# An FFN's output product two feature tiles behind its input product, in place of one

## The chip, the cores and the metric

The kernel runs on one core of a Trainium2 chip. TensorE (PE) multiplies, VectorE (DVE) and ScalarE (ACT) do the elementwise work, GpSimd (POOL) a few small things, and SyncE (SP) issues the loads. The metric is the device time of one execution in microseconds; lower is better.

## What is computed

Two layers of a decoder trunk over 256 tokens of width 1024, in float32. Each layer is an FFN, a mixer and a second FFN, each between two norms:

```
def swiglu(x, w_in, w_out):
    gate, up = jnp.split(x @ w_in, 2, axis=-1)      # w_in 1024 x 5632
    return (jax.nn.silu(gate) * up) @ w_out         # w_out 2816 x 1024
...
    h = swiglu(rms_norm(x, g[0]), ffn_w_in[layer, 0], ffn_w_out[layer, 0])
    x = x + 0.5 * rms_norm(h, g[1])
    ...                                             # mixer, then the second FFN in the same way
```

The first layer's mixer is a Mamba-2 scan beside forgetting attention, the second layer's a gated linear recurrence. So there are six phases: FFN, hybrid mixer, FFN, FFN, recurrent mixer, FFN (phases 0 to 5). The change touches the four FFNs only.

## The kernel before

The tokens are two tiles of 128. An FFN has 22 feature tiles of 128 (0 to 21). To keep float32's precision, every weight and activation is split into two parts that the fast matmul form takes exactly: a high part, made by ACT as a cast, and a low part, made by DVE as a difference. Every product is then made of three partial products.

Weights come in slabs of 512 KB: two per feature tile for the input product (below I17a, I17b and so on, from `in_ffn_in`), one for its output product (O17, from `in_ffn_out`). SP loads a slab into one of four `raw` buffers; ACT casts it into `w` (L252), DVE makes the low part (L253), and then the `raw` buffer is free for another load. Slabs are asked for in the order of first use, up to 7 slabs ahead.

The tensor engine takes its work in the order of a plan, `ffn_plan` (L42). After three tiles that are done token tile by token tile ("A"), the plan goes feature tile by feature tile. The input product of tile f, below B(f), is 32 matmuls plus their narrower companions into two PSUM buffers of the ring `rot`, which has four: the gate half first, then the up half. The output product O(f) adds tile f's part to the accumulators `side`: 12 matmuls for both token tiles, but only 6, for the first token tile, from tile 15 on, whose second token tile waits until the end (`DEFER`). Behind B(f), the chain of tile f (L530 to L541) runs on ACT and DVE: add the two parts of the gate half (`half` L267 on ACT, `sg` L268 on DVE), SiLU (`sg` L536, ACT), add the up half (`half`, `up`), multiply (`up` L538, DVE), and split the result into `hid` (L285, first ACT, then DVE). Only then can O(f) run.

In the plan, B(f) is followed by O(f-1). So the chain of f-1 has the time of one B to finish. The order on TensorE is that of the plan; on ACT and DVE a scheduler orders the casts of slabs among the chains' instructions, and each engine then works through its queue in that order, waiting at its head.

Of the kernel before, what the change touches and what calls it, by code (L numbers as in the profile page):

```python
# [8 lines left out]
F32 = mybir.dt.float32  # L9
# [7 lines left out]
P = 128          # partitions; also the rows of a token tile  # L17
NT = 2           # token tiles
DM = 1024
KT = DM // P     # contraction tiles of the model width  # L20
DFF = 2816
NF = DFF // P    # feature tiles of an FFN
HEADS = 16       # SSD heads of 64 channels
FOX = 8          # attention heads of 128 channels
EPS = 1e-6
NEG = -1e30
SLAB = 1024      # weight columns of one slab, per partition

NA = 3           # FFN feature tiles computed token tile by token tile at a phase's start
DEFER = 7        # last contraction tiles whose second token tile comes at a phase's end  # L30
LATE = {"hyb": 5, "rec": 6}  # last slabs of a mixer's output product that the phase's own pool holds
URGENT = 200     # priority of the first FFN tiles' vector work over the splits
WARM = 5         # products of ones before the first gain product: the tensor engine's clock comes up
LOOKAHEAD = {"ffn": 7, "hyb": 6, "rec": 6}     # slabs split ahead of their use

# lags in us of tensor-engine work before a product whose operand other engines still make
# [5 lines left out]
def ffn_plan(ph):  # L42
    if ph:
        plan = [("A", ph, f, t) for t in range(NT) for f in range(NA)]
    else:
        plan = [("A", ph, f, t) for f in range(NA) for t in range(NT)]
    pend, late = list(range(NA)), []

    def out(f):
        plan.append(("O", ph, f, 0))  # L50
        if f < NF - DEFER:
            plan.append(("O", ph, f, 1))
        else:
            late.append(f)

    for f in range(NA, NF):
        plan.append(("B", ph, f))
        for _ in range(2 if len(pend) > 1 else 1):
            out(pend.pop(0))
        pend.append(f)  # L60
    plan.append(("O", ph, late.pop(0), 1))
    plan += [("O", ph, NF - 1, 0), ("END", ph, 0)]
    late.append(NF - 1)
    if ph < len(PHASES) - 1:
        return plan + [("O", ph, f, 1) for f in late] + [("END", ph, 1)]
    return plan + [("O", ph, f, 1, h) for h in range(2) for f in late] + [("END", ph, 1)]
# [43 lines left out]
def hybrid_trunk(ctx: ExitStack, tc: tile.TileContext, x_in, norm_g, ffn_in, ffn_out,  # L110
# [59 lines left out]
    start_pool = tc.tile_pool(name="start", bufs=1)  # L170
    begin = start_pool.__enter__()
    g_row = begin.tile([P, DM], F32, name="g_row")   # rows that count: the first
# [47 lines left out]
    def is_late(key):  # L220
        """held until a phase's end: out of the phase's own pool"""
        what = PHASES[key[1]][0]
        return key[0] == "O" and (what == "ffn" or key[2] >= {"hyb": 16, "rec": 8}[what] - LATE[what])

# [5 lines left out]
    def behind(ins, firsts):  # L230
        """ins queues after the given instructions of its engine"""
        for h in firsts:
            if h.ins.engine == ins.ins.engine:
                tc.add_manual_dep(ins.ins, h.ins.name, mybir.DependencyInfo(
                    mybir.DependencyClass.NoSync, mybir.DependencyReason.DATA), reason="norms and splits in turn")
        return ins
# [27 lines left out]
    def halves(dst, ps):  # L264
        """dst = the two halves of ps together"""
# [4 lines left out]
    def mm_wide(ps, steps):  # L270
        """ps[:, 0:256] and ps[:, 256:512] add up to the sum of stationary^T moving, but for lo times lo;
        steps: (stationary hi, stationary lo, moving hi and lo, moving hi)"""
# [17 lines left out]
    def rstd_of(dst, ms, weight):  # L290
        """dst = weight * (mean square + EPS) ** -0.5, per token; ms holds halves of the mean square / weight ** 2"""
# [17 lines left out]
    def pre_norm(ph, t, xT, lag):  # L309
        """normalise token tile t of the residual, transpose it and split it: the input of phase ph"""  # L310
# [26 lines left out]
    def finish(ph, t, acc, weight):  # L337
        """residual update by token tile t of a phase's output, then the next phase's input"""
# [27 lines left out]
    def first_norms(xT):  # L366
        """pre_norm of the first phase: the gain is laid on all partitions by the tensor engine, and the transposes
        scale by the tokens' factors; every engine works in the order of emission"""
# [62 lines left out]
    def out_step(accs, k, t, n, act_hl, w, halves=(0, 1)):  # L431
        """accs[t][half] += act[k]^T w[k] for token tile t"""
# [10 lines left out]
    def b_one(xT, w, m=P):  # L443
        """[feature, token] of one column tile of m features"""
# [11 lines left out]
    def a_one(xT, t, s):  # L456
        """[token, column] of token tile t for 256 columns held in two slabs"""
# [12 lines left out]
    def b_tile(xT, s, off):  # L470
        """[feature, token] of the feature tile at column off of two slabs, in two halves"""
# [8 lines left out]
    def a_tile(xT, t, s):  # L480
        """[token, column] of token tile t for 256 columns held in two slabs, in two halves"""
# [11 lines left out]
    def run_ffn(ph, plan, xT, weight, hid):  # L493
        n_hid = DEFER + 2
# [55 lines left out]
    def softplus(dst, u, n, pool_):  # L550
        """dst = max(u, 0) + log(1 + exp(-|u|)), the log by its atanh series in z = e / (2 + e) <= 1/3"""
# [14 lines left out]
    def conv(src, wts, dst):  # L566
        """dst = causal convolution over the tokens of src[channel, token], taps wts[:, 0:4], bias wts[:, 4]"""
# [6 lines left out]
    def over(ap, n):  # L574
        """the same [partition, a] values for n positions of a new last axis"""
        return ap.unsqueeze(2).broadcast_to([P, ap.shape[1], n])

    def each(ap, n):
        """the same [partition, a] values for n positions of a new middle axis"""
        return ap.unsqueeze(1).broadcast_to([P, n, ap.shape[1]])  # L580

# [1 line left out]
    def run_hyb(ph, plan, xT, mp):  # L583
# [6 lines left out]
        cs = mp.tile([P, 64], F32, name="cs")               # running sums of the log decays  # L590
# [4 lines left out]
        at_pool = tc.tile_pool(name="at", bufs=1)           # until the last attention head  # L595
        at = at_pool.__enter__()
        upper = at.tile([P, P], F32, name="upper")          # 1 where partition <= column
        mask3 = at.tile([P, 3 * P], F32, name="mask3")      # causal | all | causal
# [7 lines left out]
        sd_pool = tc.tile_pool(name="sd", bufs=1)           # until the last SSD head  # L606
# [3 lines left out]
        # half the convolution, so that silu(y) = (1 + tanh(y / 2)) * (y / 2)  # L610
# [9 lines left out]
        d = sd.tile([P, NT, 24], F32, name="d")             # log decay per token: 16 SSD heads, 8 forget gates  # L620
# [9 lines left out]
        def gates(praw):  # L630
# [17 lines left out]
            # per token: columns 0:24 tile 0, 24:48 tile 1 (forget gates over both), 48:64 the SSD total of tile 0  # L648
# [8 lines left out]
            # the same with tokens along the free axis, to be laid on every partition by way of DRAM  # L657
# [8 lines left out]
        def weights_cb():  # L666
            """masked C B^T of each group and token tile, and B by token for tile 0"""
# [14 lines left out]
        def ssd(g):  # L682
            """the scan of the group's eight heads, the skip, the gate and the grouped norm"""
# [49 lines left out]
            # y holds twice the gated value, hence 4 EPS  # L733
# [71 lines left out]
        for op in plan:  # L805
# [21 lines left out]
            elif kind == "Z":  # L827
# [3 lines left out]
                # twice silu(z) = (1 + tanh(z / 2)) z  # L831
# [23 lines left out]
    def run_rec(ph, plan, xT, mp):  # L855
        gt = mp.tile([P, 8, 256], F32, name="gt")
        lr_pool = tc.tile_pool(name="lr", bufs=1)           # until the last block's gates are made
        lr = lr_pool.__enter__()
        rv = lr.tile([P, 8, 8], F32, name="rv")             # taps 0:4, conv bias, b_a, b_x, lambda
# [9 lines left out]
        dve.tensor_scalar(ls, ls, -4.0, None, op0=ALU.mult)  # half of 8 log sigmoid(lambda)  # L869
# [3 lines left out]
        def turn(c, t, ps):  # L873
            """two channel tiles of the recurrent branch from [token, channel]"""
# [12 lines left out]
        def lru(n0):  # L887
            """four blocks of channels"""
# [6 lines left out]
            for j in range(4):  # L895
# [5 lines left out]
                # sigmoid(s) = (1 + tanh(s / 2)) / 2  # L901
                act.activation(r[:, j, :], pr[:, 0:256], func=AF.Tanh, scale=0.5, bias=hb[:, n, 0:1])
                act.activation(i[:, j, :], pi[:, 0:256], func=AF.Tanh, scale=0.5, bias=hb[:, n, 1:2])
                dve.tensor_scalar(r[:, j, :], r[:, j, :], 1.0, ls[:, n:n + 1], op0=ALU.add, op1=ALU.mult)   # log a
                dve.scalar_tensor_tensor(i[:, j, :], i[:, j, :], 1.0, c[:, j, :], op0=ALU.add, op1=ALU.mult)
            act.activation(a, r, func=AF.Exp)
            # 1 - a^2 = (1 + a^2) tanh(-log a); half its root goes with 2 sigmoid
# [9 lines left out]
            # both groups' roots, then both groups' gates: a function table is loaded once for each  # L917
# [65 lines left out]
def _arrays(inp):  # L983
# [5 lines left out]
    w = a["ffn_w_in"].reshape(L, 2, 2, 4, P, 2, NF, P)          # l i kh k4 p gu f c  # L989
# [4 lines left out]
    def cols(m):                                                # column tiles, contraction split over partitions  # L994
# [3 lines left out]
    def wide(m):                                                # 256 columns in two halves of the contraction  # L998
# [6 lines left out]
    chan = lambda m, n: m.reshape(-1, n, P).transpose(2, 1, 0)  # channel tiles on partitions  # L1005
# [40 lines left out]
```

## Time and profile before

| | |
|---|---|
| time, median of 3 runs | 1071.39 us (1068.6 to 1071.75) |
| profiled execution, first to last instruction | 1069.3 us |
| its own time beside the span | not given apart; the median is 2.1 us above the span |
| TensorE busy | 1045.1 us (98%) |
| VectorE busy | 719.5 us (67%) |
| ScalarE busy | 602.9 us (56%) |
| DMA, mean over the span | 183 GB/s |

A busy TensorE is not TensorE at its peak: matmuls overlap, and a throttled clock makes them longer while the engine counts as busy. So the start times of successive products say more than the busy share.

### The profile page before, as it was taken

How to read it: one execution, taken by the hardware profiler on the slowest of the kernel's cores; microseconds unless marked ns; L12 is line 12 of the kernel's file. 1: busy time of each engine (PE TensorE's matmuls, PEld its weight loads, DVE VectorE, ACT ScalarE, POOL GpSimd, SP SyncE). 2: the span in 40 equal slices, each digit the busy share in tenths (PEclk: the TensorE clock that was granted, in tenths of full speed). 3: DMA queues.
4: the chain of work that ended last, by engine and by line, in shares of the span. 5: the costliest groups of instructions: out<-in, count | busy, mean ns of one | idle time of the engine just before them, and what ended most of it. 6: DMA issues, size and time to landing. Idle time of an engine off the chain costs nothing.

```text
span 1069.3 us, 16048 instructions
## 1 busy us (share of the span) xinstructions
PE 1045.1 (98%) x6084; PEld 912.1 (85%) x6084; DVE 719.5 (67%) x1156; ACT 602.9 (56%) x1060; POOL 24.6 (2%) x60
## 2 busy tenths in 40 slices
PE   8999999999999999999999999999999999999997
PEld 7788887999999988888887888888799878888876
DVE  7766556579888767855566675655669868655643
ACT  7655445465465556744555565445559857545531
POOL 1000000100000001000000100000010010000000
PEclk9999999999999999999999999999999999999999
DMA  7866565265645463866656285656535447665511
GB/s 269 298 227 196 188 195 171 82 219 186 202 149 168 134 226 104 289 198 197 192 181 197 83 291 185 195 193 194 185 116 178 142 154 244 232 196 193 180 59 39
DMA packets 55745, 195.90 MB, mean 183 GB/s; under 512 B 6972, under 2 KB 8148, under 8 KB 55668
## 3 DMA queue, kind: packets, MB, share of 16 engines
q1 hardware_dynamic: 52464, 190.04, 54.6%
q10 hardware_dynamic: 3204, 4.84, 1.4%
q8 instruction: 47, 0.77, 0.3%
q14 instruction: 30, 0.25, 0.1%
HBM read 193.78 MB, written 1.07 MB: 182 GB/s over the span
## 4 chain that ended last, share of the span: by engine, by line
PE 33%; DMA 30%; DVE 16%; ACT 10%; issue 8%; POOL 1%; POOLq 0%; DVEq 0%; ACTq 0%; SPq 0%
DMA raw<-in_ffn_out_dram 25%; PE rot L133 20%; PE side L133 12%; DVE w L253 10%; ACT w L252 7%; DMA raw<-in_ffn_in_dram 5%; DVE sg L268 2%; ACT junk L304 1%; DVE c L571 1%; PE rot L137 1%; DVE up L268 0%; POOL r L293 0%; DVE xn L320 0%; DMA raw<-in_rec_cols_dram 0%; DVE sc L921 0%
## 5 line engine op out<-in xcount | busy, mean ns | idle before, releaser
L253 DVE TENSOR_TENSOR w<-raw,w 128x1024 fp32r<-128x1024 f32 (+1 forms) x349 | 424.2, 1219 | 234.5 <-ACT w L252 232.7
L133 PE MATMUL rot<-xT,w 128*128 128x256 f32 (+1 forms) x3512 | 579.9, 324 | 1.3 <-DVE sg L268 1.3
L133 PEld LDWEIGHTS rot<-xT,w 128*128 128x128 f32 x3512 | 511.5, 190 | 62.0 <-DVE sg L268 1.7
L252 ACT CAST w<-raw 128x1024 fp32r<-128x1024 f32 (+1 forms) x349 | 364.8, 1049 | 220.7 <-DMA raw<-in_ffn_out_dram 177.2
L133 PE MATMUL side<-w,hid 128*128 128x512 f32 x1056 | 256.3, 393 | 8.5 <-ACT hid L285 8.4
L133 PEld LDWEIGHTS side<-w,hid 128*128 128x128 f32 x1056 | 197.3, 188 | 50.3 <-ACT hid L285 9.9
L133 PE MATMUL rot<-w,xT 128*128 128x256 f32 (+1 forms) x768 | 118.8, 313 | 0.0
L133 PEld LDWEIGHTS rot<-w,xT 128*128 128x128 f32 x768 | 105.6, 190 | 9.5 <-DVE w L253 0.3
L267 ACT COPY half<-rot 128x256 f32<-128x256 f32 x176 | 63.9, 363 | 31.8 <-PE rot L133 31.8
L285 ACT CAST hid<-up 128x256 fp32r<-128x256 f32 x76 | 30.9, 407 | 46.0 <-DVE up L538 46.0
L268 DVE TENSOR_TENSOR sg<-rot,half 128x256 f32<-128x256 f32 x100 | 41.9, 419 | 18.3 <-ACT half L267 18.2
L536 ACT ACTIVATE sg<-sg 128x256 f32<-128x256 f32 x76 | 31.8, 418 | 29.6 <-DVE sg L268 29.6
L133 PE MATMUL side<-w,os 128*128 128x512 f32 x192 | 46.2, 396 | 0.0
L133 PEld LDWEIGHTS side<-w,os 128*128 128x128 f32 x192 | 35.6, 188 | 7.9
L268 DVE TENSOR_TENSOR up<-rot,half 128x256 f32<-128x256 f32 x76 | 31.8, 418 | 9.0 <-ACT half L267 9.0
L285 DVE TENSOR_TENSOR hid<-up,hid 128x256 fp32r<-128x256 f32 x76 | 31.9, 420 | 8.5 <-ACT hid L285 8.5
L538 DVE TENSOR_TENSOR up<-sg,up 128x256 f32<-128x256 f32 x76 | 32.2, 424 | 2.0
L292 POOL TENSOR_SCALAR r<-ms 128x1 f32<-128x1 f32 x24 | 7.3, 302 | 886.6 <-ACT junk L304 881.8
L352 DVE TENSOR_TENSOR xn<-side,g_post 128x512 f32<-128x512 f32 x24 | 16.5, 691 | 15.3 <-ACT junk L304 14.9
L320 DVE SCALAR_TENSOR_TENSOR xn<-x,r,g_pre 128x512 f32<-128x512 f32 x20 | 14.1, 749 | 16.9 <-POOL r L293 16.9
L304 ACT ACTIVATE junk<-side 128x512 bf16<-128x512 f32 x24 | 14.3, 597 | 17.0 <-PE side L133 16.2
L304 ACT ACTIVATE junk<-x 128x512 bf16<-128x512 f32 x20 | 12.6, 632 | 19.5 <-DVE x L355 19.3
(195 smaller groups left out, 514.4 us busy)
## 6 DMA issues: line engine op xcount, KB each, us to landing
raw<-in_ffn_in_dram SPq DMA_DIRECT2D x176, 512.0 KB, 4.5
raw<-in_ffn_out_dram SPq DMA_DIRECT2D x88, 512.0 KB, 4.5
raw<-in_hyb_cols_dram SPq DMA_DIRECT2D x36, 512.0 KB, 4.0
raw<-in_hyb_out_dram SPq DMA_DIRECT2D x16, 512.0 KB, 3.5
raw<-in_hyb_v_dram SPq DMA_DIRECT2D x8, 512.0 KB, 3.6
raw<-in_rec_a_dram SPq DMA_DIRECT2D x8, 512.0 KB, 4.8
raw<-in_rec_cols_dram SPq DMA_DIRECT2D x8, 512.0 KB, 4.3
raw<-in_rec_out_dram SPq DMA_DIRECT2D x8, 512.0 KB, 3.6
```

Source lines behind the costliest of these rows:

```text
L133: pe.matmul(ps, lhsT=lhsT, rhs=rhs, start=start, stop=stop)
L137: pe.transpose(ps, src, ident)
L252: splits[:] = [behind(act.copy(w[:, 0, c], raw[:, c]), hold)]
L253: splits.append(behind(dve.tensor_tensor(w[:, 1, c], raw[:, c], w[:, 0, c].bitcast(F32), op=ALU.subtract), hold))
L267: act.copy(tmp, ps[:, 256:512])
L268: dve.tensor_tensor(dst, ps[:, 0:256], tmp, op=ALU.add)
L285: return act.copy(hi, src), dve.tensor_tensor(lo, src, hi.bitcast(F32), op=ALU.subtract)
L304: behind(act.activation(junk, src, func=AF.Square, scale=1.0 / (32.0 * weight), accum_out=ms[:, h:h + 1]), firsts)
L320: dve.scalar_tensor_tensor(xn[h], xt[:, cols], r, state["g_pre"][:, cols], op0=ALU.mult, op1=ALU.mult)
L352: behind(dve.tensor_tensor(hg[h], acc[h], state["g_post"][:, cols], op=ALU.mult), firsts)
L536: act.activation(sg, sg, func=AF.Silu)
L538: dve.tensor_tensor(up, sg, up, op=ALU.mult)
```

## The change

The plan lets `BEHIND` tiles, here 2, wait between input and output product: B(f) is followed by O(f-2). Ahead of the last steps, one more output product (that of tile 20) stands after the last input product. The ring of `hid` tiles grows by two buffers (9 pairs to 10). The rest of the diff only drops comments.

```
+BEHIND = 2
...
     for f in range(NA, NF):
         plan.append(("B", ph, f))
-        for _ in range(2 if len(pend) > 1 else 1):
+        for _ in range(2 if len(pend) > BEHIND else 1):
             out(pend.pop(0))
         pend.append(f)
+    while len(pend) > 1:
+        out(pend.pop(0))
     plan.append(("O", ph, late.pop(0), 1))
...
     def run_ffn(ph, plan, xT, weight, hid):
-        n_hid = DEFER + 2
+        n_hid = DEFER + BEHIND + 1
```

As slabs are asked for in the order of first use, each output slab also moves one tile back in the loads: the order after I18b is O16, I19a, I19b, O17, and at the end I21b, O19, O20, O21. Nothing moves outside the FFNs.

TensorE in phase 5, from the end of B(18) (`rot`) over the output product behind it (`side`) to the start of B(19). Before; hid_10337 and hid_10338 are the two parts of tile 17:

```order
L133 MATMUL rot_10379<-xT_8882,w_10216 128x512
L133 MATMUL side_9260<-w_10221,hid_10337 128x512 x2
L133 MATMUL side_9260<-w_10221,hid_10338 128x512
L133 MATMUL side_9261<-w_10221,hid_10337 128x512 x2
L133 MATMUL side_9261<-w_10221,hid_10338 128x512
L133 MATMUL rot_10431<-xT_8882,w_10274 128x512
```

And in the changed kernel, where hid_10251 and hid_10252 are tile 16:

```order
L136 MATMUL rot_10368<-xT_8882,w_10199 128x512
L136 MATMUL side_9260<-w_10204,hid_10251 128x512 x2
L136 MATMUL side_9260<-w_10204,hid_10252 128x512
L136 MATMUL side_9261<-w_10204,hid_10251 128x512 x2
L136 MATMUL side_9261<-w_10204,hid_10252 128x512
L136 MATMUL rot_10420<-xT_8882,w_10257 128x512
```

The product after B(18) now reads the tile whose chain began one B earlier; tile 17 (now hid_10326) is first read after B(19).

ACT in phase 5, from tile 16's last instruction to tile 17's. Before; raw_10426 is slab O20, raw_10410 I21a, raw_10479 O21, raw_10421 I21b; half_10329 and half_10333 are the gate and up half of tile 17:

```order
L285 CAST hid_10268<-up_10259 128x256
L267 COPY half_10329<-rot_10293 128x256
L252 CAST w_10428<-raw_10426 128x1024
L536 ACTIVATE sg_10327<-sg_10327 128x256
L252 CAST w_10412<-raw_10410 128x1024
L252 CAST w_10481<-raw_10479 128x1024
L267 COPY half_10333<-rot_10310 128x256
L252 CAST w_10423<-raw_10421 128x1024
L285 CAST hid_10337<-up_10328 128x256
```

In the changed kernel, with raw_10415 as O19, raw_10468 O20, raw_10399 I21a, raw_10410 I21b, raw_10479 O21, and half_10318 and half_10322 as tile 17's halves:

```order
L288 CAST hid_10251<-up_10242 128x256
L255 CAST w_10417<-raw_10415 128x1024
L270 COPY half_10318<-rot_10282 128x256
L255 CAST w_10470<-raw_10468 128x1024
L539 ACTIVATE sg_10316<-sg_10316 128x256
L255 CAST w_10401<-raw_10399 128x1024
L270 COPY half_10322<-rot_10299 128x256
L255 CAST w_10412<-raw_10410 128x1024
L255 CAST w_10481<-raw_10479 128x1024
L288 CAST hid_10326<-up_10317 128x256
```

Five casts of slabs now stand in the chain of tile 17 where four did; the fifth is O19, which had stood one chain earlier. The other three FFNs have the same pieces at the same tile.

## Rows read from the trace of the kernel before

**Rows 1.** The page: the span, and TensorE's busy time, share and instructions.

```profile
span 1069.3 us, 16048 instructions
PE 1045.1 (98%) x6084; PEld 912.1 (85%) x6084; DVE 719.5 (67%) x1156; ACT 602.9 (56%) x1060; POOL 24.6 (2%) x60
```

**Rows 2.** TensorE's waits: who for whom, us in total, times, longest.

```profile
PE side L133 <- ACT hid L285: 8.4, 4, 2.2
PE rot L133 <- DVE sg L268: 1.3, 1, 1.3
```

**Rows 3.** TensorE's timeline, phases 0, 2, 3: start, length, instructions [idle before].

```profile
152.19 5.80 PE L133 MATMUL rot<-xT,w 128*128 128x512 f32 x32
...
167.36 2.02 PE L133 MATMUL side<-w,hid 128*128 128x512 f32 x6 [2.12 <-ACT hid L285]
...
177.34 5.80 PE L133 MATMUL rot<-xT,w 128*128 128x512 f32 x32
...
550.56 5.80 PE L133 MATMUL rot<-xT,w 128*128 128x512 f32 x32
...
565.82 1.66 PE L133 MATMUL side<-w,hid 128*128 128x512 f32 x6 [2.08 <-ACT hid L285]
...
574.30 5.80 PE L133 MATMUL rot<-xT,w 128*128 128x512 f32 x32
...
739.54 5.80 PE L133 MATMUL rot<-xT,w 128*128 128x512 f32 x32
...
754.49 2.06 PE L133 MATMUL side<-w,hid 128*128 128x512 f32 x6 [2.17 <-ACT hid L285]
...
764.53 5.80 PE L133 MATMUL rot<-xT,w 128*128 128x512 f32 x32
```

**Rows 4.** The same view in phase 5, from B(17) to B(21).

```profile
1012.97 5.80 PE L133 MATMUL rot<-xT,w 128*128 128x512 f32 x32
1018.60 1.53 PE L133 MATMUL side<-w,hid 128*128 128x512 f32 x6
1019.97 5.79 PE L133 MATMUL rot<-xT,w 128*128 128x512 f32 x32
1027.79 2.25 PE L133 MATMUL side<-w,hid 128*128 128x512 f32 x6 [2.03 <-ACT hid L285]
1029.84 6.75 PE L133 MATMUL rot<-xT,w 128*128 128x512 f32 x32
...
1037.79 5.80 PE L133 MATMUL rot<-xT,w 128*128 128x512 f32 x32
...
1044.79 5.80 PE L133 MATMUL rot<-xT,w 128*128 128x512 f32 x32
```

**Rows 5.** Stretches after two waits: length, TensorE busy, granted clock, DMA share, GB/s.

```profile
566.00:568.00 2.00, 2.00 (x10) 1.00 0.86 330
...
1029.00:1031.00 2.00, 2.00 (x7) 0.50 0.00 0
```

**Rows 6.** ACT's timeline in phase 5, from O19's cast to tile 17's `hid`.

```profile
1012.34 1.05 ACT L252 CAST w<-raw 128x1024 fp32r<-128x1024 f32 x1 [3.11 <-DMA raw<-in_ffn_out_dram]
...
1020.80 1.05 ACT L252 CAST w<-raw 128x1024 fp32r<-128x1024 f32 x1 [3.18 <-DMA raw<-in_ffn_out_dram]
...
1023.97 0.35 ACT L267 COPY half<-rot 128x256 f32<-128x256 f32 x1
...
1027.34 0.40 ACT L285 CAST hid<-up 128x256 fp32r<-128x256 f32 x1 [2.07 <-DVE up L538]
```

**Rows 7.** DVE's timeline there: a low part, and tile 17's up half.

```profile
1013.43 1.22 DVE L253 TENSOR_TENSOR w<-raw,w 128x1024 fp32r<-128x1024 f32 x1 [3.16 <-ACT w L252]
...
1025.42 0.42 DVE L268 TENSOR_TENSOR up<-rot,half 128x256 f32<-128x256 f32 x1
```

**Rows 8.** SP's loads: the last two of phase 5; output slabs, us to landing.

```profile
1016.14 2.26 SPq L248 DMA_DIRECT2D raw<-in_ffn_out_dram  x2
...
raw<-in_ffn_out_dram SPq DMA_DIRECT2D x88, 512.0 KB, 4.5
```

More of the change, by code (lines that the diff above doesn't have):

```diff
@@ L29 @@
 NA = 3
+BEHIND = 2
 DEFER = 7
@@ L57, in ffn_plan @@
         plan.append(("B", ph, f))
-        for _ in range(2 if len(pend) > 1 else 1):
+        for _ in range(2 if len(pend) > BEHIND else 1):
             out(pend.pop(0))
         pend.append(f)
+    while len(pend) > 1:
+        out(pend.pop(0))
     plan.append(("O", ph, late.pop(0), 1))
@@ L493, in run_ffn @@
     def run_ffn(ph, plan, xT, weight, hid):
-        n_hid = DEFER + 2
+        n_hid = DEFER + BEHIND + 1
         hidden, accs, made, turning = {}, {}, set(), []
```

## Prediction

> **What bounds the kernel now.** First the page: TensorE is busy for 98% of the span [rows 1], so what can be won is its idle time and its slow stretches, and the other engines matter only where TensorE waits for them. Next TensorE's own list of waits. It names one wait that this change can touch: the output product (`side`) waiting for ACT's `hid`, 8.4 us in four waits of up to 2.2 us [rows 2]. Four waits and four FFNs: TensorE's timeline shows one in each, at 167.36, 565.82, 754.49 and 1027.79 us, of 2.12, 2.08, 2.17 and 2.03 us [rows 3, 4]. All four stand at the same step, O(17) behind B(18), three input products before the phase's end.
>
> What such a place costs in all is read from the starts of input products, since these take in everything. In phase 5, B(20) to B(21) is undisturbed: 1044.79 - 1037.79 = 7.00 us [rows 4]. From B(17) to B(20) should thus be 21.00 us. It is 1037.79 - 1012.97 = 24.82 in phase 5, 177.34 - 152.19 = 25.15 in phase 0, 574.30 - 550.56 = 23.74 in phase 2 and 764.53 - 739.54 = 24.99 in phase 3 [rows 3, 4]. Over by 3.82, 4.15, 2.74 and 3.99: **14.7 us in all**. The waits themselves are 8.4 of that. In phase 5 the product behind the wait, B(19), takes 6.75 us instead of 5.80 at a granted clock of 0.50, which is 1.2 GHz [rows 4, 5]; phase 2, where the clock stays at 1.00 (2.4 GHz), loses 1.1 to 1.4 us less than the others [rows 3, 5]. The rest is small stops for the second part of `hid`.
>
> Why the wait is there: ACT's timeline [rows 6]. The cast of slab O20 starts at 1020.80 after 3.18 us of idleness, and its releaser is the load of that slab. Behind it in ACT's queue stand the SiLU of tile 17, more casts, the up half (1023.97) and at last tile 17's `hid` (1027.34). The casts of O19 and O20 are 1020.80 - 1012.34 = 8.46 us apart: that loop is a load of 4.5 us [rows 8] plus the casts and low parts that give a `raw` buffer back. Three slabs per 8.46 us are enough while a tile costs TensorE an input product and two token tiles of output: 7.00 plus the second token tile's 1.37 us (one such step: 1019.97 - 1018.60 [rows 4]), or 8.37. From tile 15 on a tile costs 7.00, and ACT falls behind by some 1.4 us per tile; the time of one B no longer covers the chain.
>
> **The change part by part.** It moves work and adds none: the same matmuls, casts, low parts and loads.
>
> The waits. O(17) now stands behind B(19) instead of B(18), one input product and one output step, 7.00 us, later. The wait was 2.0 to 2.2 us, so it goes unless the chain of tile 17 gets later by about 5. Does it? Count from T, the start of the cast at the head of tile 16's chain (before: 1012.34, slab O19; after: slab O18). The order has one more cast, O19, ahead of tile 17's gate half. O19 is cast at T + 8.5, as O20 was. O20's load is issued when one more `raw` buffer is back: the last two loads of before were issued at 1016.14 and, its row ending at 1018.40 with a last issue of some 0.33, about 1018.07 [rows 8], so 1.9 apart; its cast starts at T + 10.4 rather than 8.5. Before, the up half on DVE, which frees `rot`, ended at 1025.42 + 0.42 = T + 13.5 [rows 7]; after, one cast of 1.05 us [rows 6] more stands before it: T + 14.5. O21's load needs the buffer of O19: T + 8.5 + 1.05 + 1.22 [rows 6, 7] = T + 10.8, landing 4.5 later [rows 8] at T + 15.3; its cast ends at T + 16.4, behind it `hid`, whose second part (0.43 after another low part of 1.22) is ready at about T + 18.1.
>
> TensorE, after: at the start of B(17) it has done all but O(15), a step of one token tile, 1.37 us, so B(17) starts at 1012.97 - 1.37 = 1011.60; B(19) at 1025.60, its up half 2.8 later at 1028.40 (half of 5.63, from 1012.97 to 1018.60 [rows 4]); O(17) at 1031.23. T itself: one slab fewer stands ahead of it, so it should come a third of 8.46 earlier, at 1009.5; at worst it stays at 1012.34. Then the `rot` buffer is free at 1024.0 to 1026.9 against 1028.4, and `hid` is whole at 1027.6 to 1030.5 against 1031.2. Spare: 1.5 to 4.4 and 0.7 to 3.6 us. **I take all four waits as gone.** Behind tile 17 no cast of phase 5 is left, and its last chains run with ACT idle between them, so nothing later waits either.
>
> The clock. With no stop at B(18) to B(20) I expect 1.00 there, as in phase 2 even with the wait. Bounds for its share: in phase 5, B(19) costs 6.75 - 5.80 = 0.95 and O(17) 2.25 - 1.53 = 0.72 over; over three phases that is 5 us, and by the difference to phase 2 (1.1 to 1.4 each) 3 to 4; I keep it inside the 14.7.
>
> The end of an FFN. The last chain, tile 21's, now has O(19), O(20) and O(15)'s second token tile as cover, where it had O(20) and O(15). It did not wait before: the four waits of the list [rows 2] are all accounted for. So this cover is worth 0. The first tiles: O(3) comes one tile later and its slab behind I5a and I5b, which helps those; the early wait of 1.3 us [rows 2] is for a gate half of the first tiles, ahead of every changed instruction, and stays. Two more `hid` buffers cost no time.
>
> Sum: 1069.3 - 14.7 = 1054.6 us for the profiled execution. The median lies 2.1 above that span; the runs range over 3 us, which I read in part as the clock falling in three or in four of the phases, so I carry 1.9 of the 2.1: **1056.5 us**, 1.4% less.
>
> **The rivals.**
>
> 1. The clock falls whether TensorE stops or not. Then only the waits and small stops are won: 14.7 less 3 to 5, about 10.5 us, and the time is about 1061. For it: phase 2 had the same wait without a fall [rows 5], so wait and fall are not one thing. Against it: where a row shows the fall, it follows the wait at once (1029 to 1031, the wait ending at 1027.79 [rows 4, 5]), and B(20) to B(21), without a stop, runs at its usual 7.00.
>
> 2. The change doesn't do what it says: TensorE's stop is one of buffers. Four `rot` buffers hold two tiles, so B(19) needs what tile 17 still occupies; the stop would move from O(17) to B(19) and stay at 2 us: 1071. The rows speak against it: the releaser is `hid` in all four cases, and only one wait for `rot`, of 1.3 us, is listed [rows 2]. The Trainium skill says in Perfetto Trace Analysis, section Identifying Performance Opportunities, that consistent bubbles on the engine that should be saturated can mean too little SBUF or PSUM for the next tile. By that rule this rival would be the first guess, at no gain; the trace's releasers don't agree with it.
>
> 3. Slower: the two output slabs in one chain. If O20's load gets its buffer only after O19's low part, it is issued at T + 10.8 and lands at T + 15.3. SiLU, I21a's cast and the up half follow, and the `rot` buffer is free at about T + 19.5. With T at its worst, 1012.34, that is 1031.8, against 1028.4: a stop of 3.4 us inside B(19), and with half clock behind it 1.7 more (0.95 + 0.72 above), 5.1 per FFN, where 3.7 were lost. Four times 1.4 is 5.7 us more than before: 1077. It decides at T + 16.1, from which on B(19) has to wait. Against it: the order of buffers read from the issues of before (1.9 apart).
>
> **How the numbers follow.** Forecast 0.83, rival 1 0.08, rival 2 0.05 (to be read as no change), rival 3 0.04. A change below 0.3% can't be told from none here. Faster takes forecast and rival 1, 0.91; same 0.05; slower 0.04. The range: 1053.5, if the whole 14.7 and the lowest run's offset come together, to 1061.5, which takes in rival 1; the rest, 9 in 100, lies outside, with some for the offset.
>
> **What would show it.** The list of TensorE's waits has no row of `side` for `hid`, or one below 1 us. B(17) to B(20) takes 21.0 us in all four FFNs, and the granted clock is 1.00 through them. ACT still idles some 3 us for the load of an output slab each tile; it only no longer matters. Wrong would be: a wait of `rot` for DVE's `up` or `sg` in B(19) (rivals 2 and 3), falls of the clock elsewhere (rival 1), or a span above 1062.

## The result and the profile after

The changed kernel takes 1056.78 us (median of 4 runs, 1054.86 to 1059.34) against 1071.57 before (1068.6 to 1073.87): ratio 0.985, 95% interval 0.982 to 0.988. The forecast was 1056.5. The profiled execution spans 1056.5 us; its own time is 1058.17, which is 1.4 above the median.

The first view to look at is TensorE's list of waits (who for whom, us in total, times, longest):

```profile
PE rot L140 <- DVE xn L323: 2.2, 1, 2.2
PE side L136 <- ACT hid L288: 1.6, 1, 1.6
PE side L136 <- ACT pT L792: 1.3, 3, 0.6
...
PE side L136 <- DVE dg L387: 0.7, 1, 0.7
```

Of the output product's 8.4 us in four waits [rows 2], 1.6 us in one are left, and that one is not at O(17). TensorE's timeline in phase 5, from B(17) to B(20) (start, length, instructions; the x32 of a row are all of an input product, 16 matmuls of 512 columns and 16 of 256):

```profile
1002.59 5.80 PE L136 MATMUL rot<-xT,w 128*128 128x512 f32 x32
1008.22 1.53 PE L136 MATMUL side<-w,hid 128*128 128x512 f32 x6
1009.59 5.80 PE L136 MATMUL rot<-xT,w 128*128 128x512 f32 x32
1015.22 1.53 PE L136 MATMUL side<-w,hid 128*128 128x512 f32 x6
1016.59 5.80 PE L136 MATMUL rot<-xT,w 128*128 128x512 f32 x32
1022.22 1.53 PE L136 MATMUL side<-w,hid 128*128 128x512 f32 x6
1023.59 5.80 PE L136 MATMUL rot<-xT,w 128*128 128x512 f32 x32
```

Three cycles take 1023.59 - 1002.59 = 21.00 us, where they took 24.82 [rows 4]. Phase 0 has the same, from 149.44 to 170.44:

```profile
149.44 5.80 PE L136 MATMUL rot<-xT,w 128*128 128x512 f32 x32
...
170.44 2.74 PE L136 MATMUL rot<-xT,w 128*128 128x512 f32 x15
```

(The length of the second row is cut by the window that was asked for; its start counts.) Phase 2 goes from 543.45 to 564.45 and phase 3 from 731.84 to 752.84, again 21.00 us each. The granted clock through the four places, and in the one place where it fell while TensorE worked (stretch, length, TensorE busy, clock, DMA share, GB/s):

```profile
150.00:180.00 30.00, 30.00 (x165) 1.00 0.66 208
556.00:584.00 28.00, 26.37 (x138) 1.00 0.68 215
744.00:766.00 22.00, 22.00 (x121) 1.00 0.73 238
1008.00:1037.00 29.00, 29.00 (x159) 1.00 0.15 52
860.00:864.00 4.00, 3.46 (x12) 0.57 0.00 0
```

ACT's timeline in phase 5 from O18's cast to tile 17's `hid` answers to [rows 6]:

```profile
1002.11 1.05 ACT L255 CAST w<-raw 128x1024 fp32r<-128x1024 f32 x1 [3.42 <-DMA raw<-in_ffn_out_dram]
...
1010.32 1.05 ACT L255 CAST w<-raw 128x1024 fp32r<-128x1024 f32 x1 [3.21 <-DMA raw<-in_ffn_out_dram]
1011.28 0.36 ACT L270 COPY half<-rot 128x256 f32<-128x256 f32 x1
1012.51 1.05 ACT L255 CAST w<-raw 128x1024 fp32r<-128x1024 f32 x1 [0.87 <-DMA raw<-in_ffn_out_dram]
1013.47 0.41 ACT L539 ACTIVATE sg<-sg 128x256 f32<-128x256 f32 x1
...
1014.73 0.36 ACT L270 COPY half<-rot 128x256 f32<-128x256 f32 x1
...
1016.23 1.06 ACT L255 CAST w<-raw 128x1024 fp32r<-128x1024 f32 x1 [0.19 <-DMA raw<-in_ffn_out_dram]
1017.91 0.41 ACT L288 CAST hid<-up 128x256 fp32r<-128x256 f32 x1 [0.63 <-DVE up L541]
```

And DVE's, answering to [rows 7]:

```profile
1016.00 0.42 DVE L271 TENSOR_TENSOR up<-rot,half 128x256 f32<-128x256 f32 x1
...
1018.93 0.41 DVE L288 TENSOR_TENSOR hid<-up,hid 128x256 fp32r<-128x256 f32 x1
```

ACT is no faster: it still idles 3.2 us for an output slab (1010.32) with tile 17's chain behind it, and tile 17's `hid` is whole only at 1018.93 + 0.41 = 1019.34. That is 4.1 us after the end of B(18) at 1015.22. The wait has not been worked off; TensorE merely asks for this tile at 1022.22, when it has been there for 2.9 us. The page's chain of work that ended last shows it too: loads of output slabs are 25% of it before and 6% after.

The balance between the two spans: 14.7 us at the four places, and 1.4 us in the first phase, where TensorE's wait of 1.3 us for `sg` is absent. (The wait for `dg` is 1.1 us shorter too, but it ends no earlier, at 7.83 against 7.73 us, so nothing is won there.) Both waits stand ahead of every product that was moved, and they differ from one execution of a kernel to the next. Against that, 1.6 us go for `hid` at the end of phase 2, 0.7 us more at the wait for `xn` after the recurrent mixer, and 1.3 us with the fall of the clock behind it. (At the end of that wait the two kernels are 870.85 - 860.54 = 10.31 us apart. At B(17) of phase 5 they are 1012.97 - 1002.59 = 10.38 apart, of which 1.37 is O(15), which now stands later, so 9.01 are left.) Together 12.5; the spans differ by 12.8.

### The profile page after: what moved, and what is told of

Same layout as the page of the kernel before. It is cut to its first block, busy times and chain, and to the rows that moved or that the text cites. A ratio compares the mean times of both kernels' runs of the same rounds, so it can differ in the third digit from the quotient of the medians.

```text
span 1056.5 us, 16049 instructions
## 1 busy us (share of the span) xinstructions
PE 1041.4 (99%) x6084; PEld 910.7 (86%) x6084; DVE 717.9 (68%) x1156; ACT 600.3 (57%) x1060; POOL 24.5 (2%) x60
## 4 chain that ended last, share of the span: by engine, by line
PE 75%; DVE 8%; DMA 8%; ACT 4%; issue 4%; POOL 1%; DVEq 0%; POOLq 0%; ACTq 0%; SPq 0%
PE rot L136 49%; PE side L136 25%; DMA raw<-in_ffn_out_dram 6%; DVE w L256 4%; ACT w L255 2%; DMA raw<-in_ffn_in_dram 2%; PE rot L140 1%; DVE c L574 1%; DVE sg L271 1%; ACT junk L307 1%; DVE sc L924 0%; PE side L140 0%; DVE hid L288 0%; DVE up L271 0%; POOL r L296 0%
## 5 line engine op out<-in xcount | busy, mean ns | idle before, releaser
L255 ACT CAST w<-raw 128x1024 fp32r<-128x1024 f32 (+1 forms) x349 | 364.5, 1048 | 218.6 <-DMA raw<-in_ffn_out_dram 176.9
L307 ACT ACTIVATE junk<-side 128x512 bf16<-128x512 f32 x24 | 14.3, 597 | 20.6 <-PE side L136 19.7
L323 DVE SCALAR_TENSOR_TENSOR xn<-x,r,g_pre 128x512 f32<-128x512 f32 x20 | 14.1, 749 | 16.8 <-POOL r L296 16.8
L136 PE MATMUL side<-w 128*128 128x512 f32 x96 | 23.3, 402 | 1.1 <-DVE w L288 1.1
```

The lines of the kernel that those rows point to most:

```text
L136: pe.matmul(ps, lhsT=lhsT, rhs=rhs, start=start, stop=stop)
L255: splits[:] = [behind(act.copy(w[:, 0, c], raw[:, c]), hold)]
L307: behind(act.activation(junk, src, func=AF.Square, scale=1.0 / (32.0 * weight), accum_out=ms[:, h:h + 1]), firsts)
L323: dve.scalar_tensor_tensor(xn[h], xt[:, cols], r, state["g_pre"][:, cols], op0=ALU.mult, op1=ALU.mult)
```

## Experiments

Theory A: O(17) waited because ACT's queue stands at the cast of an output slab, whose load comes out of a loop of four `raw` buffers that turns slower than TensorE from tile 15 on; distance in TensorE's order covers that. Rivals: the stop is one of PSUM buffers (B), it is the later loads that help (C), the clock falls on its own account (D). Each ratio below is to the kernel before as measured on the same chip, with medians of 1071.89, 1073.07 and 1072.72 us on the three chips.

**The loop, attacked directly.** The kernel before, one tile behind, with a fifth `raw` buffer for the FFNs' output slabs alone:

```
-            raw = rawp.tile([P, SLAB], F32, name="raw", bufs=4)
+            own = late and PHASES[key[1]][0] == "ffn"
+            raw = (pools[key[1]] if own else rawp).tile([P, SLAB], F32, name="rawo" if own else "raw",
+                                                        bufs=1 if own else 4)
```

> Kernel before (output product one tile behind), but the output slabs of the FFNs get a raw buffer of their own, a fifth one. Theory A (tile 17's chain is late because ACT's queue stands at the cast of an output slab, and the loop of four raw buffers takes 8.5 us where TensorE needs 7.0): output slab's load is issued 1.5 us earlier in each turn, the loop gets shorter than 7.0 to 7.5, and the four waits of the output product for hid shrink to under 0.5 us each: about 1057 to 1061 us. Rival B (the stop is of PSUM buffers or is there whatever ACT does): four waits of 2 us stay, 1071.

Measured: 1061.13 us, 0.990 of before (0.987 to 0.994), just above what was expected and 10.8 us below the kernel before. ACT's timeline in phase 5, the casts of four successive output slabs:

```profile
972.96 1.05 ACT L253 CAST w<-rawo 128x1024 fp32r<-128x1024 f32 x1 [2.81 <-DMA rawo<-in_ffn_out_dram]
978.94 1.05 ACT L253 CAST w<-rawo 128x1024 fp32r<-128x1024 f32 x1 [1.15 <-DMA rawo<-in_ffn_out_dram]
984.92 1.05 ACT L253 CAST w<-rawo 128x1024 fp32r<-128x1024 f32 x1 [0.16 <-DMA rawo<-in_ffn_out_dram]
990.78 1.05 ACT L253 CAST w<-rawo 128x1024 fp32r<-128x1024 f32 x1 [0.61 <-DMA rawo<-in_ffn_out_dram]
```

These come 5.9 us apart, where the casts of O19 and O20 were 8.46 apart [rows 6]. On average it is 6.4 over the last 21 output slabs of the phase, where it was 8.3 in the kernel before (eleven turns from 929.71 to 1020.80). The idle time before the four is 0.2 to 2.8 us. In the chain of tile 17 the cast of an output slab has no idle time ahead of it, since its load has landed:

```profile
1010.31 1.05 ACT L253 CAST w<-rawo 128x1024 fp32r<-128x1024 f32 x1
```

TensorE's waits in that kernel:

```profile
PE side L133 <- ACT hid L286: 2.1, 4, 1.3
PE rot L137 <- DVE xn L321: 1.6, 1, 1.6
```

The four waits of 2 us at O(17) are gone without any change in TensorE's order, and from B(17) to B(20) the four FFNs take 21.00, 21.00, 21.31 and 21.14 us: 0.45 over in all, where it was 14.7. What is left of the waits, 2.1 us, stands at other tiles (the longest, 1.3 us, at 495.70), presumably since one B covers the chain with little to spare. The gain is not the whole one: the next version wins 16.7 us on the same chip. The cause is the loop, as A has it; B expected no change. One point of the expectation fell short: one wait is longer than 0.5 us. One thing is not taken apart: with the loop, the casts' places in ACT's queue moved as well, and a kernel that only puts the chain ahead of the casts was not run.

**The two halves of the change apart.** TensorE two behind, slabs asked for in the order of before (here and below, `ffn_plan` takes the distance as an argument):

```
-    for plan in plans:
-        for op in plan:
+    for ph, what in enumerate(PHASES):
+        for op in ffn_plan(ph, 1) if what[0] == "ffn" else plans[ph]:
```

> Changed kernel, but the slabs are asked for in the order of the kernel before; only TensorE's order is two tiles behind. Theory A: the distance in TensorE's order is what covers the chain, so all four waits are gone and the time is that of the changed kernel, 1055 to 1059. Rival C (what helps is that output slabs are loaded one tile later): the waits stay, 1071.

Measured: 1055.23 us, 0.985 (0.980 to 0.989). The whole gain is there. And the other half, TensorE one behind with the loads of the changed kernel:

```
-        plans.append({"ffn": ffn_plan, ...
+        plans.append({"ffn": lambda p: ffn_plan(p, 1), ...
-    for plan in plans:
-        for op in plan:
+    for ph, what in enumerate(PHASES):
+        for op in ffn_plan(ph, 2) if what[0] == "ffn" else plans[ph]:
```

> Kernel before, but the slabs are asked for in the order of the changed kernel; TensorE stays one tile behind. Theory A: O(17) still waits for hid after one B, and one more cast stands in tile 17's chain, so the waits are as before or 1 to 2 us longer: 1071 to 1077. Rival C: the waits go, 1057.

Measured: 1076.61 us, 1.004 (1.002 to 1.006): slower than before. TensorE's timeline in phase 0 of it:

```profile
151.73 5.79 PE L136 MATMUL rot<-xT,w 128*128 128x512 f32 x32
...
158.30 1.20 PE L136 MATMUL side<-w,hid 128*128 128x512 f32 x4 [0.30 <-DVE hid L288]
159.34 5.79 PE L136 MATMUL rot<-xT,w 128*128 128x512 f32 x32
167.69 3.37 PE L136 MATMUL side<-w,hid 128*128 128x512 f32 x6 [2.56 <-ACT hid L288]
```

So the later loads alone win nothing, and C falls. In phase 0 the wait is longer (2.56 us, where it was 2.12 [rows 3]), and in phase 2 too (2.67 against 2.08). But in phase 5 it is 2.15 against 2.03, and in phase 3 only 0.4 us and 0.6 us for the second part of `hid` are left of 2.17:

```profile
757.77 0.73 PE L136 MATMUL side<-w,hid 128*128 128x512 f32 x2 [0.43 <-ACT hid L288]
759.06 1.18 PE L136 MATMUL side<-w,hid 128*128 128x512 f32 x4 [0.56 <-DVE hid L288]
```

The wait goes with where ACT stands: the first cast in tile 17's chain that waits for an output slab starts 8.64, 9.07, 5.98 and 7.78 us after B(17) in phases 0, 2, 3 and 5. That fits A. From B(17) to B(20) the four places are over by 5.21, 6.87, 1.54 and 3.19 us, 16.8 in all against 14.7. Since single places lose more or less than before, it is not shown that the fifth cast is what makes this kernel slower.

**The four places one by one.** Two behind in phases 0 and 3 only:

```
-        plans.append({"ffn": ffn_plan, ...
+        plans.append({"ffn": lambda p: ffn_plan(p, {0: 2, 2: 1, 3: 2, 5: 1}[p]), ...
```

> Two tiles behind in phases 0 and 3 only, one behind in phases 2 and 5. Theory A: each FFN's place is a loss of its own, 4.15 and 3.99 us are won and 2.74 and 3.82 stay: 1071.5 - 8.1 = 1063.4, with waits for hid of some 2 us at O(17) of phases 2 and 5 only, and the clock falling behind these alone. Rival D (the clock falls whether or not TensorE stops): falls in phases 0 and 3 too, only 4.3 to 5 us won, about 1067.

Measured: 1065.06 us, 0.993 (0.991 to 0.996), a gain of 4.4 to 10.1 us; 8.1 lies inside, and so does D's 5. The profile decides. Granted clock in phase 0, phase 2, phase 3 and phase 5:

```profile
160.00:180.00 20.00, 20.00 (x111) 1.00 0.67 215
563.00:566.00 3.00, 3.00 (x11) 0.54 0.69 223
740.00:770.00 30.00, 30.00 (x165) 1.00 0.71 222
1024.00:1030.00 6.00, 5.19 (x14) 0.50 0.00 0
```

TensorE's waits there, in phases 2 and 5:

```profile
562.10 1.99 PE L136 MATMUL side<-w,hid 128*128 128x512 f32 x6 [2.23 <-ACT hid L288]
...
1024.81 2.92 PE L136 MATMUL side<-w,hid 128*128 128x512 f32 x6 [3.59 <-ACT hid L288]
```

Where the wait went, the clock stays at 2.4 GHz; where it stayed, the clock is at 1.2 GHz around and behind it. D falls. From B(17) to B(20), phases 2 and 5 lose more here than in the kernel before (4.70 and 8.07 us over, against 2.74 and 3.82). But the profiled execution, with 1069.92 us, is the slowest of the ten (1060.25 to 1069.92), so it doesn't say why the median gain, 6.8 us, is below the middle of the forecast.

**Where the distance is needed.** One behind up to tile 14, two from there:

```
-        for _ in range(2 if len(pend) > BEHIND else 1):
+        keep = BEHIND if f > 14 else 1
+        for _ in range(min(2, len(pend) - keep + 1)):
```

> One tile behind up to tile 14 as in the kernel before; B(15) and B(16) then follow each other, and from there on the output product is two behind. Theory A: only the stretch from tile 15 on, where a tile costs TensorE 7.00 us, needs the distance, so the time is that of the changed kernel, 1055 to 1059, and no wait for hid is left there. Rival B (PSUM buffers): with two input products in a row TensorE stops for rot, 1 us or more in each FFN, and 4 us or more are lost against the changed kernel.

Measured: 1055.16 us, 0.983 (0.980 to 0.986): all of the gain. B(15) and B(16) run as one block, without a stop for `rot` (phase 0):

```profile
135.98 11.44 PE L137 MATMUL rot<-xT,w 128*128 128x512 f32 x64
147.25 2.89 PE L137 MATMUL side<-w,hid 128*128 128x512 f32 x12
```

11.27 us from start to start is twice 5.63. Four PSUM buffers are thus enough even for this, and rival B is out a second time. Two waits for `hid` of 0.4 us are left at earlier tiles, which are still one tile behind.

**More distance, and more cover at the end.** `BEHIND = 3`:

> Three tiles behind in place of two. Theory A: the chain of tile 17 is covered already by two, so nothing more is won in the middle; at the end one more output product, 1.36 us, covers tile 21's chain: as the changed kernel or up to 1.5 us faster, 1054 to 1058. If distance itself were worth something (a rival to A), another 5 us or more would go.

Measured: 1057.91 us, 0.985 (0.982 to 0.989), as the changed kernel; no wait for `hid` is listed at all. And one more output step ahead of O(21):

```
-    plan.append(("O", ph, late.pop(0), 1))
+    for _ in range(2):
+        plan.append(("O", ph, late.pop(0), 1))
```

> Changed kernel with one more output step (tile 16's second token tile, 1.36 us) ahead of the last one, O(21). Theory A: the wait of 1.6 us for tile 21's hid in phase 2 is the old delay of ACT coming back at the end of the phase; with 1.36 us more of cover it shrinks to about 0.3, and up to 1.5 us are won: 1055 to 1057. Rival E: the step is missed behind the phase's end, where it covers the norm, and each of the five boundaries loses up to 1.4 us: 1060 to 1063.

Measured: 1060.24 us, 0.987 (0.983 to 0.991). The wait at tile 21 is not there (nor is it in the repeat of the changed kernel below, so this is not the step's doing for certain), but TensorE now stops behind the phase's end, three times (after phases 0, 2, 3), as here:

```profile
202.36 0.50 PE L137 MATMUL rot<-w,xT 128*128 128x256 f32 x2 [0.24 <-ACT xT L289]
203.08 7.23 PE L137 MATMUL rot<-w,xT 128*128 128x256 f32 x58 [0.23 <-DVE xT L289]
```

That is about 1.4 us over the three places, so E is right in kind, a third of its size. The rest of that execution's excess is a wait of 2.1 us for `sg` in the first phase with a fall of the clock behind it, which the edit does not touch. The intervals overlap: whether this version is slower than the changed kernel stays open; it is not faster. The same step on top of TensorE's order alone:

> TensorE two tiles behind, slabs asked for in the order of the kernel before, and the one more output step ahead of O(21). Theory A: the 0.9 and 0.2 us that tile 21's hid still cost go, and nothing else changes: 1054 to 1056, within 0.2% of the version without the step.

Measured: 1059.62 us, 0.987 (0.983 to 0.990), with the same stops. This is a miss, since 1054 to 1056 was expected, and the stops of 1.4 us explain only part of it.

**Side by side.** Three versions on one chip. The changed kernel again:

> The changed kernel once more, on the chip of the two versions beside it: 0.985 of the kernel before, some 1056 to 1057 us.

Measured: 1055.64 us, 0.983 (0.980 to 0.987). The wait at tile 21 in phase 2 is not in this execution's list, and no wait for `hid` is listed. Two from tile 14 on:

> Two behind from tile 14 on only, once more. Theory A: no difference to the changed kernel but for the wait at tile 21's hid in phase 2 (1.6 us there, none here), so 0 to 2 us faster than it.

Measured: 1056.64 us, 0.984 (0.980 to 0.988): no difference to the changed kernel beside it. And two behind together with the output slabs' own buffer (the first experiment's edit, with `n_hid = DEFER + 2`):

> Changed kernel with the output slabs' own raw buffer (and 9 pairs of hid in place of 10, which makes room for it). Theory A: both remove the same waits, so the gains don't add: 1054 to 1058, as the changed kernel; ACT's idle time for output slabs shrinks all the same. A rival (each removes something else): 10 us less than the changed kernel, 1046.

Measured: 1054.3 us, 0.982 (0.979 to 0.985), all six runs within 1053.6 to 1054.8. The gains don't add: both remove the same waits. ACT's idle time for output slabs shrinks from 176.9 us in the changed kernel to 95.2, as expected. It has the lowest median and the narrowest spread, but against the changed kernel's interval the difference of 1.3 us is not shown.

## Why the prediction was right

- **The loss per place** (3.82, 4.15, 2.74 and 3.99 us, 14.7 in all), read from the starts of input products: each place now takes 21.00 us, so the whole sum came back.
- **Part of the hit is luck.** The forecast median is met within 0.3 us, but the profiled span, forecast at 1054.6, is 1056.5: the losses of 1.6, 0.7 and 1.3 us in the balance were not in the sum, and the 1.4 us of the first phase, which were not in it either, made up for some of them. The median then lay only 0.3 us above that span, where 1.9 had been carried.
- **The chain of tile 17 gets later, but not by 5 us.** This was worked out for phase 5 alone, and there it holds: T was put between B(17)'s start less 2.1 us and plus 0.7; it is 1002.11, 0.5 us ahead of B(17). The `rot` buffer is free at 1016.42, T + 14.3 (14.5 worked out); `hid` is whole at T + 17.2 (18.1). Spare: 2.9 us at O(17), inside the 0.7 to 3.6. The other FFNs were not worked out, and they differ: T lies 2.3 us ahead of B(17) in phase 0, but 2.2 us behind it in phase 2 and 0.3 in phase 3, and the spare is 5.0, 0.1 and 2.1 us. In phase 2, tile 17's `hid` is whole at 562.57 + 0.42 = 562.99, and O(17) starts at 563.08 (ACT, DVE, TensorE):

```profile
561.55 0.41 ACT L288 CAST hid<-up 128x256 fp32r<-128x256 f32 x1 [0.87 <-DVE up L541]
562.57 0.42 DVE L288 TENSOR_TENSOR hid<-up,hid 128x256 fp32r<-128x256 f32 x1
563.08 1.53 PE L136 MATMUL side<-w,hid 128*128 128x512 f32 x6
```

  That the wait of phase 2 is gone was thus close, below the stated spare. In the repeat of the changed kernel the same place has 2.3 us (561.34 against 563.62).
- **Rival 2** spoke of PSUM buffers, and these were not short. But a buffer was, one step further back: a fifth `raw` buffer in SBUF removes the four waits, though `hid` is named as the releaser.
- **The clock** stays at 2.4 GHz through the four places, and the two-phase version ties the falls to the waits, which a single trace had not settled. A fall of the clock elsewhere was named as a sign of being wrong, and one came, behind the wait for `xn`; it too follows a stop, so it doesn't speak for rival 1.
- **What was mis-sized: the last chain.** "So this cover is worth 0", and nothing later waits, did not hold in the profiled execution: O(21) of phase 2 waits 1.6 us, which is more than the 1 us that was named as the limit for such a row. TensorE's timeline (start, length, instructions, idle before):

```profile
577.08 4.27 PE L136 MATMUL side<-w,hid 128*128 128x512 f32 x18
582.99 8.49 PE L136 MATMUL side<-w,hid 128*128 128x512 f32 x36 [1.63 <-ACT hid L288]
```

  The prediction had read the last tiles of phase 5, the only FFN with no phase behind it, where "no cast of phase 5 is left". In phase 2 two casts of the next phase's slabs stand in each of the last chains, and ACT needs 582.53 - 561.55 = 20.98 us from tile 17's `hid` to tile 21's:

```profile
582.53 0.41 ACT L288 CAST hid<-up 128x256 fp32r<-128x256 f32 x1 [1.81 <-DVE up L541]
```

  TensorE asks for O(21) some 18.1 us after O(17) (563.08 to 577.08, and 18 matmuls or 4.1 us more). So the first part of `hid` has 2.9 us less to spare at tile 21 than at tile 17. In phase 2 tile 17's first part was ready 1.1 us ahead of O(17) (561.55 + 0.41 against 563.08), so tile 21's came too late. In phase 3, with the same casts, it was 3.2 us ahead, and in phase 2 of the changed kernel's repeat 3.3; in neither is a wait listed, and with three behind there is none.
- **The early wait of 1.3 us** "stays", the prediction said. It was absent in this execution, and over all executions of these kernels it ranges from nothing to 2.2 us. It stands ahead of every product that was moved, so it is not the change's doing either way; how much of the runs' spread it makes is not shown.

## What to carry to other kernels

When the saturated engine waits for a chain of other engines, look what stands at the head of their queues: here a cast waiting for a load, put ahead of the chain by the scheduler. Distance in the saturated engine's order covers such a delay without removing it, and it is needed only where that engine's period drops below the loader's loop (here 7.00 against 8.46 us); the other cure, one more buffer in that loop, removes the four waits by itself. A spare that was worked out in one phase need not hold in the others: it was 5.0, 0.1, 2.1 and 2.9 us in the four FFNs. Read what a stop costs from the starts of successive equal pieces, not from the wait alone: 14.7 us, where the waits sum to 8.4.

## What the runs showed of the hardware

Stops of 2 us can cost more than themselves. The granted clock of 0.50, which is 1.2 GHz, followed the waits of 2.12, 2.17 and 2.03 us of the kernel before, but not the one of 2.08 us in phase 2 [rows 3, 5]; in the changed kernel it followed a wait of 2.18 us for `xn`:

```profile
860.54 1.97 PE L140 MATMUL rot<-ident,xn 128*128 128x128 f32 x8 [2.18 <-DVE xn L323]
862.16 2.00 PE L136 MATMUL side<-w 128*128 128x512 f32 x4
```

The same wait of 2.0 us in the repeat of the changed kernel had a fall behind it as well. In the kernel before it is 1.5 us and with the slabs' own buffer 1.6 us, without a fall; but with the later loads alone, 1.7 us were followed by one (stretch behind it, length, TensorE busy, clock, DMA share, GB/s):

```profile
875.00:877.00 2.00, 2.00 (x6) 0.50 0.00 0
```

And with three behind, a wait of 2.2 us for `sg` had none. So of equal waits of some 2 us one brings the clock down and another does not, from one execution to the next.

That the fast matmul form takes both parts exactly, as said of the kernel before, is what its comments say; no run here measures it.
